# Token loads, product order and half norms of a two-layer diffusion trunk

## The chip, the core and the metric

The kernel runs on one core of one Trainium2 chip. The metric is the device time of one execution in microseconds (us).

## What is computed

One inference step of a diffusion trunk with two layers of width 2048, for 512 latent (sample) and 128 context (prompt) tokens, all in fp32. Each layer normalizes, scales and shifts its input, projects it, runs two mixers with gates, and projects their joined output back into the residual.

```python
def even_mixer(h, w_in, w_out, ...):        # layer 0; layer 1 is odd_mixer, built alike
    qa, ka, va, ga, ub, bb, cb, gb = split_cols(h @ w_in, EVEN_SPLIT)
    q = rms_norm(q_heads(qa, A_KV, A_GROUP), qn)
    ...
    o = banded_attend(apply_rope(q, cos, sin), apply_rope(k, cos, sin), v, ctx[0], ctx[1], sink_g)
    y_a = merge_heads(o) * jax.nn.silu(ga)
    y_b = gated_short_conv(ub, bb, cb, conv_w) * jax.nn.silu(gb)
    return jnp.concatenate([y_a, y_b], axis=-1) @ w_out, new
```

The change touches the projection by `w_out` in both layers, the one by the odd layer's `w_in`, the norm between the layers, and the norm of the queries (`q_heads`).

## The kernel before

All 640 tokens are worked on together. Activations lie transposed, features on the 128 partitions and tokens along the row, so a matrix of 2048 features is 16 tiles of 128x640, and a matmul takes 320 tokens, one of two halves, at a time. Weights stream from memory. [...] A program-wide scheduler takes the written program and orders the instructions of each engine, so that a line's place in the source is not its place in time; buffers come from pools, with a semaphore wait where one is still in use.

`project` does an output projection, and the front of the odd input projection. It starts with three output tiles at once (`run_tiles`), quarter by quarter of the 16 input tiles in the order 0, 2, 1, 3. The four token tiles of a quarter, a unit below, are made by `make_h` just before their use: a tile `yin` of the mixers' output is loaded from memory on SyncE's queue and split into `h`. After that comes one output tile by itself, and the rest goes in pairs (`run_pairs`): two output tiles by two token halves form a 2x2 block product over two halves of the inputs, done with seven products instead of eight from sums of weights and of token tiles. Each product has 24 matmuls. Q1, P6, P7 and P4 add up in one PSUM bank, `pa`; N5 and Q3 share `pb0`; Q2 opens `pb1`. `after` copies what a product leaves for later (L507, L510, L512 for `u2` after P6, L516 for `u3` after P7) and passes finished blocks to `out`. There are 20 pairs: 6 in layer 0's output projection, 8 in the odd layer's front, 6 in layer 1's output projection. Weight sums for them are made on VectorE in place (`sx`, `sf`).

Between the layers, `x1_last` squares the last residual tiles and `norm_half` forms the mean square of one token half with one-column matmuls against `ones`, takes the power on GpSimd, broadcasts it with matmuls against `ident`, and copies it out; only then can the next layer's token tiles of that half be scaled and split (L1318, L1320, L1322).

`q_gen` (it holds L643) norms and rotates the queries while other projections' matmuls run; each `yield` hands the turn to these.

Of the kernel before, what the change touches and what calls it, by code (L numbers as in the profile page):

```python
# [50 lines left out]
def trunk_kernel(ctx: ExitStack, tc: tile.TileContext, I: dict, O: dict):  # L51
# [24 lines left out]
    def close(name):  # L76
        pools.pop(name).__exit__(None, None, None)
# [224 lines left out]
    def drain(queue):  # L302
        while queue:
            advance(queue, 1)
# [139 lines left out]
    def run_pairs(cols, w_ap, mov, room, begin, out, tail):  # L444
# [81 lines left out]
        for i, (p, name) in enumerate(seq):  # L526
# [100 lines left out]
    def q_gen(ap, pp, tag, gain, then=None, wait=True):  # L627
# [11 lines left out]
        V.tensor_add(m, m, sw)  # L639
        yield  # L640
        ss = psT()
# [215 lines left out]

    def y_maker(tags, width, held=()):
        def make(k):
            if k in held:  # L860
                drain(attn)
                t = y[k]
            else:
                t = pools["cur"].tile([P, width], F32, tag=tags[k % len(tags)], name="yin", bufs=4 // len(tags))[:, 0:NT]
                nc.sync.dma_start(t, ydram[k])
            hi, lo = new_h(k)
            split(hi, lo, t)
        return make

# [252 lines left out]

    def late_yin(k):
        t = pools["cur"].tile([P, NT], F32, tag="xr", name="yin", bufs=3)
        nc.sync.dma_start(t, ydram[k])
        split(*new_h(k), t)

    def half_of(k0, i):  # L1130
# [5 lines left out]

    def project(w, cols, n0, maker, job, begin, out, tail, by_half=False):

        go_on = run_tiles([(cols[n], job(n)) for n in range(3)], w, maker, order=(0, 2, 1, 3), by_half=by_half)

# [36 lines left out]

    def project_out(l, maker, finish, last, tail):

# [33 lines left out]

        project(W_OUT[l], [n * P for n in range(KT)], n0, maker, job, begin, out, tail)


    make_y0 = y_maker(("q0h", "q0l", "q1h", "q1l"), NT)

    def mid_tile(n):
        return pools["cur"].tile([P, NT], F32, tag=n, name=n, bufs=1)  # L1220

    def y0_maker(k):
        if k < 4:
            return make_y0(k)
        if k == 8:
            close("even")
            open_pool("mid")
            lay_out("T7 T6 T5 T4 sf xr w8 sx")
            st["acc"], st["sq"] = (mid_tile(n) for n in ("acc", "sq"))
            attn.append(forms())  # L1230
        late_yin(k)

# [11 lines left out]
    def x1_last(t, h):  # L1244
        n, sl = KT - 2 + t, HV[h][1]
        if t != h:
            squares(n, sl)
            return
        nc.gpsimd.dma_start(xdram[n], st["xr", n])
        if h:  # L1250
            g = norm_half(n, h)
            advance([g], 1)
            advance([g], 1)
            drain(prep)
            attn.append(g)
        else:
            prep.append(norm_half(n, h))


    def norm_half(n, h):  # L1260
        sl = HV[h][1]
        A.activation(st["sq"][:, sl], st["xr", n][:, sl], AF.Square)
        yield
        starts = [HALF * h, HALF * h + P, HALF * (h + 1) - P]
# [3 lines left out]
        for i, s in enumerate((st["acc"], st["sq"])):  # L1268
            for b, o in enumerate(starts):
                PE.matmul(tot[:, 4 * i + b:4 * i + b + 1], s[:, o:o + P], ones[:, 0:1], start=True, stop=True)  # L1270
# [26 lines left out]

    project_out(0, y0_maker, x1_done, x1_last, x1_tail)

# [273 lines left out]


    def y1_maker(k):
        if k == 4:
            drain(attn)
            close("odd")
            open_pool("fin")
            lay_out("T7 T6 xr T5 w8 sx sf T4")  # L1580
            attn.append(forms())
        if k % 8 >= 4:
            late_yin(k)
        else:
            t = pools["cur"].tile([P, 768], F32, tag="P", name="yin", bufs=P_BUFS)[:, 0:NT]
            nc.sync.dma_start(t, ydram[k])
            split(*new_h(k), t)

# [12 lines left out]
    def rows_last(t, h):  # L1601

        n = KT - 2 + t
        if not t:
            if h == 0:
                prep.append(rows_later(n))
            return
# [11 lines left out]

    project_out(1, y1_maker, rows_out, rows_last, lambda name: None)  # L1620
    close("fin")
# [48 lines left out]
```

## Time and profile before

| | before |
|---|---|
| median of 3 runs | 2295.69 us (2292.07 to 2299.78) |
| the profiled execution | 2294.4 us |
| its span | 2292.6 us |
| mean granted clock of TensorE | 0.999 |
| TensorE matmuls busy | 2255.9 us (98%) |
| VectorE / ScalarE / GpSimd busy | 1589.8 / 1088.9 / 160.0 us |
| mean traffic | 150 GB/s |

Rows of a timeline read: start in us, length in us, engine, line, operation, what it writes <- what it reads, shapes, and in brackets the idle time of the engine before it with what ended it. A matmul's length is about twice the distance to the next one, since they overlap: distances between starts tell the pace. Rows of the waits read: who waited for whom, us in total, times, longest. Rows of windows give the stretch, its length, busy us and instructions (x) of TensorE's matmuls, its weight loads, VectorE, ScalarE and GpSimd, then the granted clock, the DMA engines' share and GB/s.

### The profile page before, as it was taken

What the parts mean: (1) busy time and instruction counts of PE and PEld (TensorE: products, weight loads), DVE (VectorE), ACT (ScalarE), POOL (GpSimd) and SP (SyncE); (2) the same over time, 40 slices, a digit from 0 to 9 for tenths busy, and PEclk for the clock granted to TensorE, in tenths of its full rate; (3) what the DMA queues carried; (4) which work ended last, traced back from release to release, by engine and by line L of the source; (5) the groups of instructions that cost most, each with busy time, mean ns of one, the idle gap of its engine ahead of it and who ended that gap; (6) DMA issues with size and microseconds to landing.
All of it is one profiled execution on the core that took longest, in us unless ns stands there. A gap on an engine that the chain in (4) does not pass through costs nothing.

```text
span 2292.6 us, 41100 instructions
## 1 busy us (share of the span) xinstructions
PE 2255.9 (98%) x15900; PEld 2178.0 (95%) x15900; DVE 1589.8 (69%) x2831; ACT 1088.9 (47%) x2304; POOL 160.0 (7%) x224
## 2 busy tenths in 40 slices
PE   7999999999999999999999999999999999999999
PEld 5889999999999999999999999999999999999999
DVE  4666968779779776887787665365665655557775
ACT  5325652443522222544464443465565676755443
POOL 1001000000000000000100001011111100000101
PEclk9999999999999999999999999999999999999999
DMA  9985537547367564854553335223223221238642
GB/s 321 294 270 161 158 113 218 152 133 219 116 210 216 177 191 137 277 173 140 164 155 108 116 118 152 79 60 104 79 63 101 71 60 49 76 101 269 184 138 62
DMA packets 380899, 342.89 MB, mean 150 GB/s; under 512 B 16402, under 2 KB 338416, under 8 KB 380192
## 3 DMA queue, kind: packets, MB, share of 16 engines
q1 hardware_dynamic: 366288, 296.00, 43.0%
q0 software_dynamic: 13696, 42.10, 5.4%
q8 instruction: 125, 2.05, 0.4%
q10 hardware_dynamic: 720, 2.16, 0.3%
q14 instruction: 70, 0.57, 0.1%
HBM read 301.27 MB, written 38.93 MB: 148 GB/s over the span
## 4 chain that ended last, share of the span: by engine, by line
PE 85%; DVE 4%; ACT 4%; DMA 3%; issue 3%; POOL 1%; SPq 0%; ACTq 0%; POOLq 0%; DVEq 0%
PE pq L537 7%; PE pq L536 7%; PE pq L535 7%; PE pa L256 6%; PE pa L257 6%; PE pb L256 6%; PE pa L258 6%; PE pb L257 6%; PE pb L258 6%; PE pb L271 2%; PE pb L270 2%; PE pa L270 2%; PE pb L272 2%; PE pa L272 2%; PE pa L271 2%
## 5 line engine op out<-in xcount | busy, mean ns | idle before, releaser
L220 ACT ACTIVATE wh<-raw 128x512 fp32r<-128x512 f32 (+1 forms) x456 | 273.1, 600 | 574.0 <-PE pb L257 406.9
L221 DVE TENSOR_TENSOR wl<-raw,wh 128x512 fp32r<-128x512 f32 (+1 forms) x456 | 295.7, 650 | 212.3 <-ACT wh L220 191.9
L256 PE MATMUL pa<-h,wh 128*128 128x320 f32 x1024 | 325.3, 319 | 4.3 <-ACT h L220 2.0
L257 PE MATMUL pa<-h,wh 128*128 128x320 f32 x1024 | 319.5, 313 | 1.7 <-DVE h L221 0.8
L258 PE MATMUL pa<-h,wl 128*128 128x320 f32 x1024 | 318.2, 311 | 0.9 <-DVE wl L221 0.9
L257 PE MATMUL pb<-h,wh 128*128 128x320 f32 x1024 | 317.1, 310 | 0.0
L258 PE MATMUL pb<-h,wl 128*128 128x320 f32 x1024 | 316.8, 309 | 0.0
L256 PE MATMUL pb<-h,wh 128*128 128x320 f32 x1024 | 316.6, 310 | 0.0
L198 DVE SCALAR_TENSOR_TENSOR acc<-adaw,sT,acc 128x1024 f32<-128x1024 f32 x240 | 299.7, 1276 | 0.0
L256 PEld LDWEIGHTS pa<-h,wh 128*128 128x128 f32 x1024 | 193.1, 189 | 18.3 <-issue 10.0
L257 PEld LDWEIGHTS pa<-h,wh 128*128 128x128 f32 x1024 | 193.3, 189 | 7.6 <-issue 3.3
L535 PE MATMUL pq<-h,wh 128*128 128x320 f32 x640 | 198.7, 311 | 0.4 <-ACT wh L220 0.4
L537 PE MATMUL pq<-h,wl 128*128 128x320 f32 x640 | 198.0, 309 | 0.1
L536 PE MATMUL pq<-h,wh 128*128 128x320 f32 x640 | 197.7, 309 | 0.0
L258 PEld LDWEIGHTS pa<-h,wl 128*128 128x128 f32 x1024 | 193.1, 189 | 3.5 <-issue 2.1
L257 PEld LDWEIGHTS pb<-h,wh 128*128 128x128 f32 x1024 | 192.2, 188 | 1.0 <-issue 0.8
L256 PEld LDWEIGHTS pb<-h,wh 128*128 128x128 f32 x1024 | 192.1, 188 | 0.8 <-issue 0.4
L258 PEld LDWEIGHTS pb<-h,wl 128*128 128x128 f32 x1024 | 192.3, 188 | 0.0
L537 PE MATMUL pq<-T,wl 128*128 128x320 f32 x480 | 147.7, 308 | 0.2 <-DVE wl L221 0.2
L536 PE MATMUL pq<-T,wh 128*128 128x320 f32 x480 | 147.9, 308 | 0.0
L535 PE MATMUL pq<-T,wh 128*128 128x320 f32 x480 | 147.6, 308 | 0.1
L270 PE MATMUL pa<-h,wh 128*128 128x320 f32 x432 | 141.0, 326 | 0.0
(431 smaller groups left out, 5306.0 us busy)
## 6 DMA issues: line engine op xcount, KB each, us to landing
adaw<-in_ada_w SPq DMA_DIRECT2D x128, 512.0 KB, 4.3
raw<-in_ev_w_in SPq DMA_DIRECT2D x176, 256.0 KB, 3.5
raw<-in_od_w_in SPq DMA_DIRECT2D x160, 256.0 KB, 2.9
ada<-in_ada_w SPq DMA_DIRECT2D x32, 1024.0 KB, 7.9
w<-in_od_w_in SPq DMA_DIRECT2D x24, 512.0 KB, 4.0
yd<-y POOLq DMA_DIRECT2D x32, 320.0 KB, 3.2
yin<-yd SPq DMA_DIRECT2D x32, 320.0 KB, 4.5
w<-yd SPq DMA_DIRECT2D x32, 320.0 KB, 4.2
```

Source lines behind the costliest of these rows:

```text
L198: V.scalar_tensor_tensor(out=acc[c], in0=w, scalar=sT[:, kt, c:c + 1], in1=acc[c], op0=ALU.mult, op1=ALU.add)
L220: A.activation(hi, x, AF.Copy)
L221: V.tensor_sub(lo, x, hi)
L256: PE.matmul(ps, wh[:, i, :], hi[:, sl], start=(j == js[0] if alone else (pos == 0 and j == 0)), stop=False)
L257: PE.matmul(ps, wh[:, i, :], lo[:, sl], start=False, stop=False)
L258: last_mm[0] = PE.matmul(ps, wl[:, i, :], hi[:, sl], start=False, stop=(j == js[1] - 1 if alone else (pos == 3 and j == 3)))
L270: PE.matmul(ps, wh[:, j, :], hi[:, sl], start=(qd == 0 and j == 0), stop=False)
L271: PE.matmul(ps, wh[:, j, :], lo[:, sl], start=False, stop=False)
L272: PE.matmul(ps, wl[:, j, :], hi[:, sl], start=False, stop=(qd == 3 and j == 3))
L535: PE.matmul(ps, wh[:, j, :], hi, start=(new and h == 0 and j == 0), stop=False, **kw)
L536: PE.matmul(ps, wh[:, j, :], lo, start=False, stop=False, **kw)
L537: PE.matmul(ps, wl[:, j, :], hi, start=False, stop=(h == 1 and j == 3), **kw)
```

## The change

Four edits, all of order, place and time of issue; no arithmetic is added or taken away.

1. Token loads. `late_yin` and `y_maker` go. A new callback `ahead` of `run_tiles`, called one unit early, loads tiles 8 to 11 into the buffers of attention's probabilities ("P", four of them) and tiles 4 to 6, later 12 to 14, into the three `xr` buffers. It also closes the layer's pool and opens the next before quarter 1; formerly that came with tile 8 in layer 0 and with tile 4 in layer 1. Tiles 7 and 15 are loaded when they are split.
2. Pairs. Q2 moves from fourth to sixth: Q1, N5, P6, P7, Q3, Q2, P4. The next pair's A21 is loaded after P7, A12 and A22 after Q3.
3. Queries. `q_gen` yields once more between the square and the matmuls on it.
4. Norm between the layers. With Q3 earlier, the first half's norm starts a product earlier; the second half's sums are issued behind the latest matmul and its work is spread over more turns. The first residual tiles come back at P7 instead of Q2, except the fourth.

```diff
-        MOV = {"Q1": "B11", "N5": "T1", "P6": "T2", "Q2": "B21", "P7": "T3", "Q3": "B22", "P4": "T4"}
+        MOV = {"Q1": "B11", "N5": "T1", "P6": "T2", "P7": "T3", "Q3": "B22", "Q2": "B21", "P4": "T4"}
...
             elif name == "P7":
+                load(p + 1, "A21")
+            elif name == "Q3":
                 load(p + 1, "A12")
-            elif name == "Q3":
-                load(p + 1, "A21")
                 load(p + 1, "A22")
-            if name in ("Q2", "P7") and p == len(cols) - 1:
+            if name in ("P7", "Q2") and p == len(cols) - 1:
                 tail(name)
...
         V.tensor_add(m, m, sw)
-        yield
+        for _ in range(2):
+            yield
         ss = psT()
...
-    def late_yin(k):
-        t = pools["cur"].tile([P, NT], F32, tag="xr", name="yin", bufs=3)
-        nc.sync.dma_start(t, ydram[k])
-        split(*new_h(k), t)
...
+    def y_ahead(old, new, tags, then=None):
+        def ahead(qd, js):
+            if qd == 2:
+                for k in range(8, 12):
+                    yin_load(k, *P_PLACE)
+                return
+            if qd == 1:
+                drain(attn)
+                close(old)
+                open_pool(new)
+                lay_out(tags)
+                if then:
+                    then()
+                attn.append(forms())
+            for k in range(4 * qd, 4 * qd + 3):
+                yin_load(k, "xr", 3)
+        return ahead
...
     def y0_maker(k):
-        if k < 4:
-            return make_y0(k)
-        if k == 8:
-            close("even")
-            open_pool("mid")
...
-        late_yin(k)
+        yin_split(k, *(("q0h", "q0l", "q1h", "q1l")[k], 1) if k < 4 else ("xr", 3))
...
     def x1_last(t, h):
         n, sl = KT - 2 + t, HV[h][1]
+        if h:
+            nc.gpsimd.dma_start(xdram[n], st["xr", n])
         if t != h:
             squares(n, sl)
-            return
-        nc.gpsimd.dma_start(xdram[n], st["xr", n])
-        if h:
+        elif h:
+            drain(prep)
             g = norm_half(n, h)
-            advance([g], 1)
-            advance([g], 1)
-            drain(prep)
+            next(g)
             attn.append(g)
...
     def norm_half(n, h):
...
-        yield
+        for _ in range(1 + h):
+            yield
...
-            for b, o in enumerate(starts):
-                PE.matmul(tot[:, 4 * i + b:4 * i + b + 1], s[:, o:o + P], ones[:, 0:1], start=True, stop=True)
+            with tc.issue_after(last_mm[0].ins) if h else ExitStack():
+                for b, o in enumerate(starts):
+                    PE.matmul(tot[:, 4 * i + b:4 * i + b + 1], s[:, o:o + P], ones[:, 0:1], start=True, stop=True)
...
     def x1_tail(name):
-        if name == "Q2":
-            for k in range(4):
-                x1_back(k, big("w8", bufs=4))
+        for k in (0, 1, 2) if name == "P7" else (3,):
+            x1_back(k, big("w8", bufs=4))
...
-        if k % 8 >= 4:
-            late_yin(k)
...
+        yin_split(k, *P_PLACE if k < 4 else ("xr", 3))
```

Two places show what the scheduler makes of it. The first is TensorE's order at the end of P6 in the last pair of layer 0. `T_` tiles are sums of token tiles (P6, P7), `h_` tiles are token tiles. Before, Q2 follows, and only its 24 matmuls later P7:

```order
L535 MATMUL pq<-T_11054,wh 128x320
L536 MATMUL pq<-T_11054,wh 128x320
L537 MATMUL pq<-T_11054,wl 128x320
L535 MATMUL pq<-h_10678,wh 128x320 [waits Activation_49]
L536 MATMUL pq<-h_10678,wh 128x320
L537 MATMUL pq<-h_10678,wl 128x320 [waits DVE_49]
L535 MATMUL pq<-h_10683,wh 128x320
```

Now:

```order
L536 MATMUL pq<-T_11078,wh 128x320
L537 MATMUL pq<-T_11078,wl 128x320
L535 MATMUL pq<-h_10670,wh 128x320 [waits Activation_49]
L536 MATMUL pq<-h_10670,wh 128x320
L537 MATMUL pq<-h_10670,wl 128x320 [waits DVE_49]
L535 MATMUL pq<-h_10673,wh 128x320
L536 MATMUL pq<-h_10673,wh 128x320
L537 MATMUL pq<-h_10673,wl 128x320
L535 MATMUL pq<-h_10676,wh 128x320
L535 MATMUL pq<-T_10760,wh 128x320 [waits Activation_49]
L536 MATMUL pq<-T_10760,wh 128x320
```

Seven matmuls of Q3 stand between P6 and P7; the other 17 of Q3 follow P7. The wait for ScalarE ahead of P7 holds the copy of `u2` as well as the weights' split.

The second is TensorE's order at the norm of the second token half, where the next layer has begun (`pa`, `Sp` and `pb` are its first output tiles; `r` is the power's result, broadcast over the partitions). Before:

```order
L258 MATMUL pa<-h_12945,wl 128x320
L1281 MATMUL T<-ident,r_12880 128x128 [waits PE_49,Pool_49]
L1281 MATMUL T<-ident,r_12880 128x128
L1281 MATMUL T<-ident,r_12880 128x64
L257 MATMUL pa<-h_12945,wh 128x320
L258 MATMUL pa<-h_12945,wl 128x320
L257 MATMUL Sp<-h_12933,wh 128x320
L258 MATMUL Sp<-h_12933,wl 128x320
L256 MATMUL Sp<-h_12937,wh 128x320
L257 MATMUL Sp<-h_12937,wh 128x320
L258 MATMUL Sp<-h_12937,wl 128x320
```

Six more rows into `Sp` follow there, then the first into `pb`. Now:

```order
L1281 MATMUL T<-ones,sq 128x1 [waits DVE_49]
L1281 MATMUL T<-ones,sq 128x1 x2
L258 MATMUL pa<-h_12933,wl 128x320
L257 MATMUL Sp<-h_12929,wh 128x320
L258 MATMUL Sp<-h_12929,wl 128x320
L256 MATMUL Sp<-h_12933,wh 128x320
L257 MATMUL Sp<-h_12933,wh 128x320
L258 MATMUL Sp<-h_12933,wl 128x320
L1292 MATMUL T<-ident,r_12951 128x128 [waits Pool_49]
L1292 MATMUL T<-ident,r_12951 128x128
L1292 MATMUL T<-ident,r_12951 128x64
L256 MATMUL pb<-h_12921,wh 128x320 [waits Activation_49]
```

The broadcast of `r` has moved from ahead of thirteen wide matmuls to directly ahead of the first `pb` matmul, and its sums (`ones`) stand six wide matmuls ahead of it. The sums of the first half and their broadcast, which stood in P4 and behind it, now stand in Q2, with P4's 24 matmuls behind them.

More of the change, by code (lines that the diff above doesn't have):

```diff
@@ L856, in save_y, with yin_load, yin_split @@
             nc.gpsimd.dma_start(ydram[k], y[k])
[L858 to L864, printed above, removed]
-                nc.sync.dma_start(t, ydram[k])
-            hi, lo = new_h(k)
-            split(hi, lo, t)
-        return make
+    yin = {}
+    def yin_load(k, tag, bufs, n=NT):
+        yin[k] = pools["cur"].tile([P, n], F32, tag=tag, name="yin", bufs=bufs)[:, 0:NT]
+        nc.sync.dma_start(yin[k], ydram[k])
+    def yin_split(k, *place):
+        if k not in yin:
+            yin_load(k, *place)
+        split(*new_h(k), yin.pop(k))
     xTm = [sp.tile([P, 4 * NT + 1], F32, name=f"xT{g}") for g in range(4)]
@@ L1135, in form_of, with project @@
         return lambda j: (T[j][:, 0, i * HALF:(i + 1) * HALF], T[j][:, 1, i * HALF:(i + 1) * HALF])
-    def project(w, cols, n0, maker, job, begin, out, tail, by_half=False):
-        go_on = run_tiles([(cols[n], job(n)) for n in range(3)], w, maker, order=(0, 2, 1, 3), by_half=by_half)
+    def project(w, cols, n0, maker, job, begin, out, tail, by_half=False, ahead=None):
+        go_on = run_tiles([(cols[n], job(n)) for n in range(3)], w, maker, order=(0, 2, 1, 3), by_half=by_half,
+                          ahead=ahead)
         quarters = [(cols[n], qd) for n in range(3, n0) for qd in range(4)]
@@ L1176, in project, with project_out @@
         drain(prep)
-    def project_out(l, maker, finish, last, tail):
+    def project_out(l, maker, ahead, finish, last, tail):
         n0 = N_SINGLE[l]
@@ L1212, in out, with mid_places @@
             seen.add(n)
-        project(W_OUT[l], [n * P for n in range(KT)], n0, maker, job, begin, out, tail)
-    make_y0 = y_maker(("q0h", "q0l", "q1h", "q1l"), NT)
+        project(W_OUT[l], [n * P for n in range(KT)], n0, maker, job, begin, out, tail,
+                ahead=ahead)
     def mid_tile(n):
         return pools["cur"].tile([P, NT], F32, tag=n, name=n, bufs=1)
-    def y0_maker(k):
-        if k < 4:
-            return make_y0(k)
-        if k == 8:
-            close("even")
-            open_pool("mid")
-            lay_out("T7 T6 T5 T4 sf xr w8 sx")
-            st["acc"], st["sq"] = (mid_tile(n) for n in ("acc", "sq"))
-            attn.append(forms())
-        late_yin(k)
+    def y_ahead(old, new, tags, then=None):
[15 more added lines that the diff above has]
+        return ahead
+    def mid_places():
+        st["acc"], st["sq"] = (mid_tile(n) for n in ("acc", "sq"))
+    P_PLACE = ("P", P_BUFS, 640)
+    y0_ahead = y_ahead("even", "mid", "T7 T6 T5 T4 sf xr w8 sx", mid_places)
+    def y0_maker(k):
+        yin_split(k, *(("q0h", "q0l", "q1h", "q1l")[k], 1) if k < 4 else ("xr", 3))
     def squares(n, sl=slice(0, NT)):
@@ L1572, in trunk_kernel @@
     advance(attn, 1)
+    y1_ahead = y_ahead("odd", "fin", "T7 T6 xr T5 w8 sx sf T4")
     def y1_maker(k):
[L1576 to L1581, printed above, removed]
-        if k % 8 >= 4:
-            late_yin(k)
[L1584 to L1587, printed above, removed]
+        yin_split(k, *P_PLACE if k < 4 else ("xr", 3))
     def rows_out(n):
@@ L1604, in rows_last @@
         if not t:
-            if h == 0:
+            if h:
                 prep.append(rows_later(n))
```

5 lines of the change are left out of this document (2 added, 3 removed).

## Prediction

> **What bounds the kernel now.** I read the engine totals first, then the chain that ended last, then what TensorE (PE) waited for, and only then the timeline at the places that the change touches.
>
> ```profile
> span 2292.6 us, 41100 instructions
> PE 2255.9 (98%) x15900; PEld 2178.0 (95%) x15900; DVE 1589.8 (69%) x2831; ACT 1088.9 (47%) x2304; POOL 160.0 (7%) x224
> PE 85%; DVE 4%; ACT 4%; DMA 3%; issue 3%; POOL 1%; SPq 0%; ACTq 0%; POOLq 0%; DVEq 0%
> PE pa L256 <- ACT h L220: 2.0, 3, 0.8
> PE pa L256 <- DVE gg L1004: 1.6, 1, 1.6
> PE pa L257 <- DVE h L221: 0.8, 3, 0.4
> PE pq L535 <- ACT wh L220: 0.4, 1, 0.4
> ```
>
> PE is busy 98% of the span and carries 85% of the chain. The last four lines are waits of its matmuls (total, times, longest): a token tile's high part (L220) or low part (L221) cost 2.8 us in six waits, and the pairs' products (pq) lost 0.4 us in one. So the change, which leaves the matmuls' number alone, can win only stretches in which PE stands or runs slowly, and can lose by making new ones. The profiled execution took 2294.4 us, 1.8 outside the span; the median of the runs is 2295.7. I count against 2294.4 and put the difference on the median. About 0.3%, 6.9 us, is what a measurement can tell from no change.
>
> **Tokens of layer 0's output projection.** These rows of the PE timeline are the starts around five stalls (start, length, operation, idle time and its releaser).
>
> ```profile
> 926.39 0.31 PE L258 MATMUL pa<-h,wl 128*128 128x320 f32 x1
> 927.14 0.41 PE L256 MATMUL pa<-h,wh 128*128 128x320 f32 x1 [0.44 <-ACT h L220]
> 928.00 0.41 PE L257 MATMUL pa<-h,wh 128*128 128x320 f32 x1 [0.45 <-DVE h L221]
> ...
> 941.28 0.31 PE L258 MATMUL pb<-h,wl 128*128 128x320 f32 x1
> 942.29 0.42 PE L256 MATMUL pa<-h,wh 128*128 128x320 f32 x1 [0.70 <-ACT h L220]
> 942.54 0.31 PE L256 MATMUL pb<-h,wh 128*128 128x320 f32 x1
> 942.69 0.31 PE L258 MATMUL pa<-h,wl 128*128 128x320 f32 x1
> ...
> 952.36 0.31 PE L258 MATMUL pa<-h,wl 128*128 128x320 f32 x1
> 952.90 0.42 PE L257 MATMUL pa<-h,wh 128*128 128x320 f32 x1 [0.22 <-DVE h L221]
> 953.15 0.31 PE L258 MATMUL pa<-h,wl 128*128 128x320 f32 x1
> 954.28 0.42 PE L256 MATMUL pa<-h,wh 128*128 128x320 f32 x1 [0.82 <-ACT h L220]
> 954.53 0.31 PE L257 MATMUL pb<-h,wh 128*128 128x320 f32 x1
> ```
>
> A matmul that waits for nothing starts 0.15 us after the one before it (942.54 to 942.69). Against that the five stalls cost 0.60, 0.71, 0.86, 0.39 and 0.98 us from start to start, 3.54 together, and the matmul behind each comes 0.25 instead of 0.15 later (942.29 to 942.54), some 0.4 more: 3.9. Behind them stand loads:
>
> ```profile
> 941.50 0.74 ACT L220 ACTIVATE h<-yin 128x640 fp32r<-128x640 f32 x1 [2.67 <-DMA yin<-yd]
> 897.41 23.45 SPq L233 DMA_DIRECT2D raw<-in_ev_w_out  x7
> 920.95 1.41 SPq L1127 DMA_DIRECT2D yin<-yd  x3
> ```
>
> ScalarE (ACT) had nothing to do until the token tile had landed, and SyncE's queue (SP) stood 23.45 us at the weights ahead of it, so the first late tiles were asked for at 920.95. In the new order tiles 8 to 11 go to attention's buffers, ahead of those weights; 4 to 6 are asked for at about 921, one unit (the four tiles of one quarter of the rows) before their use at 942, which no landing in these rows overruns. Only tiles 7 and 15 still wait until a buffer is free. I leave one stall of 0.5 us for those and count **-3.4** (ends: -3.9, and -1.9 if both stall like the longest, 0.98). In layer 1 tiles 0 to 3 and 8 to 11 had such places already, and the six waits quoted above leave it about 0.1 us: **-0.1**. The 1.6 us behind gg comes from attention and stays.
>
> **The six products' order.** Formerly Q2's 24 matmuls, in another bank, lay between P6 and P7, which share one. Now P7 must not write before ACT has copied P6's result out (L512), and the new order has only seven matmuls of Q3 between them in 18 of the 20 pairs, five in layer 0's first and two in layer 1's first.
>
> ```profile
> 1012.62 0.31 PE L537 MATMUL pq<-T,wl 128*128 128x320 f32 x1
> 1012.76 0.31 PE L535 MATMUL pq<-h,wh 128*128 128x320 f32 x1
> ...
> 1012.81 0.63 ACT L220 ACTIVATE wh<-sf 128x512 fp32r<-128x512 f32 x1 [1.13 <-PE pq L536]
> 1013.35 0.41 ACT L512 COPY tables<-pq 128x320 f32<-128x320 f32 x1
> ```
>
> P6 ends with the first row, and ACT splits a weight tile before it copies; the copy ends at 1013.76, 1.00 us after the following product's first start. Seven matmuls take 7 x 0.147 = 1.03 us, so the cover is just spent. But P7's weight load waits with it, and behind a wait the next start came 0.10 us late above: I take 0.11 a pair. Five matmuls cover 0.73 and two 0.29, which leaves 0.4 and 0.85. Sum: 18 x 0.11 + 0.4 + 0.85 = **+3.3**. The low end is 0 (the copy goes first, 0.6 us after P6); the high end is one more split of 0.63 ahead of the copy, 12.6 on top. Behind the wait on PE's queue are P7 and everything after, so nothing hides it.
>
> [...]
>
> The loads that change places with it are free as far as these rows tell: A21 and A12 only swap, P7's weights are summed together with P6's, and Q3's in-place sum now has one product between it and P6's splits, where N5's to P6 had none and pq lost 0.4 us in all.
>
> **The norm between the layers.** With Q3 a product earlier, the first token half's norm (mean square by one-column matmuls into T, power on GpSimd (POOL), L1281's broadcast, then ACT copy, VectorE (DVE) scale, ACT split) moves ahead of P4.
>
> ```profile
> 1123.54 0.72 PE L1270 MATMUL T<-ones,acc 128*128 128x1 f32 x6
> 1125.24 0.72 PE L1270 MATMUL T<-ones,sq 128*128 128x1 f32 x6
> 1127.21 0.86 PE L1281 MATMUL T<-ident,r 128*128 128x128 f32 x6
> 1128.96 1.19 PE L1270 MATMUL T<-ones,sq 128*128 128x1 f32 x6 [0.88 <-ACT sq L1262]
> 1130.01 0.88 PE L256 MATMUL pa<-h,wh 128*128 128x320 f32 x2
> 1131.79 0.64 PE L257 MATMUL pa<-h,wh 128*128 128x320 f32 x1 [0.63 <-DVE h L1322]
> 1136.76 0.78 PE L1281 MATMUL T<-ident,r 128*128 128x128 f32 x6
> 1137.34 0.39 PE L257 MATMUL pa<-h,wh 128*128 128x320 f32 x1
> 1139.33 0.52 PE L256 MATMUL pb<-h,wh 128*128 128x320 f32 x2
> ...
> 1130.00:1140.00 10.00, 9.37 (x47) 8.79 (x48) 5.46 (x15) 3.53 (x8) 3.96 (x5) 0.70 1.14 374
> ```
>
> From 1123.54 to 1139.33 are 15.79 us. In them stand 48 wide matmuls (7.05) and six small groups of 0.58 (1136.76 to 1137.34; 3.5), so 5.2 us were lost: about half as idle time, the other half at the lower clock (0.70 in the last row, a stretch of 10 us: 47 matmuls, where 68 fit at 0.147).
>
> Afterwards: the first broadcast needs 1.97 us from its last sum's start (1125.24 to 1127.21), and behind the sum's 0.58 five wide matmuls cover 0.73, so 0.66 is exposed. P4's 24 matmuls (3.5) then cover the way to the first token tiles, which took 2.8 here (1127.21 to 1130.01). The second half's power has six matmuls (0.88) where it needs some 1.4 to 1.5: 0.6. Its way from broadcast to the first pb matmul takes 1.99 us (1137.34 to 1139.33), which thirteen matmuls covered; now pb comes at once: 1.99 exposed. Together 3.25 against 5.2, a gain of 1.95 at full clock. Whether the clock falls again is open. It fell here among stalls of 0.88 and 0.63, and did not behind a longer one alone:
>
> ```profile
> 2070.62 0.31 PE L272 MATMUL pb<-h,wl 128*128 128x320 f32 x1
> 2072.57 0.42 PE L256 MATMUL pa<-h,wh 128*128 128x320 f32 x1 [1.64 <-DVE gg L1004]
> 2072.98 0.31 PE L258 MATMUL pa<-h,wl 128*128 128x320 f32 x1
> ```
>
> The new stalls lie between these cases. I charge a third of the same drop, 0.95: **-1.0**. Ends: -4.7 (the 1.99 and the clock both come out hidden) and +2 (the drop in full, and POOL's token stores of 0.7 each ahead of the second power).
>
> **The query's squares** (matmuls of qsq into T, L643) wait for a split low part, as this row of the waits has it:
>
> ```profile
> PE T L643 <- DVE ptl L221: 1.4, 3, 0.5
> ```
>
> Three waits, 1.4 us, and with the 0.10 us behind each about 1.7. The squares come one step later now, so those that waited have more time; but in the new order the matmuls after attention's transposes are placed differently too, and a wait can form at the work that follows on the squares (root, rotary). I take about a third, **-0.5** (ends: -1.7 with all three gone, and +1, two waits of the longest kind, 0.5, for nothing won).
>
> The sum is -3.4 - 0.1 + 3.3 - 1.0 - 0.5 = -1.7: 2292.7 for the profiled execution, 2294.0 on the median.
>
> **The rivals.** *All of it hides* (chance 0.18): copies go early (0), tokens -3.9, norm -4.7, squares -1.7, layer 1 -0.1: -10.4, 2285.3. For it: a copy that goes ahead of its split ends at 0.6 us, well inside the cover; against it: in the rows the split goes first, and cover and copy are then equal to 0.03 us. *The copy is late* (0.13): in every pair ACT has one more split ahead of L512. P7 then waits 20 x 0.63 = 12.6 longer: 2306.6. The sign turns where the waits at P7 reach 5.0 us (3.3 + 1.7), 0.25 a pair, and they tell from no change at 11.9 (8.6 more), 0.6 a pair. For it: the copy stood behind one split already; against it: a second split needs a weight buffer that only matmuls behind P7 would free. *The clock stays up* (0.16): the norm wins its 1.95: 2293.0. [...] *The change does nothing where it was meant* (0.13): tiles land as late as before, since the early loads push the weights on SP's queue back by as much, so the -3.4 is missing: 2297.4. The order speaks against it: SP stood there 23 us anyway. The forecast itself has 0.40.
>
> **How the numbers follow.** The range runs from 2285, the first rival's value, to 2304, between the forecast and the late copy. Faster than 2288.8 is the first rival with a little of the others, 0.2; slower than 2302.6 the second with its milder forms, 0.14; the rest 0.66.
>
> **What would show it.** Right: no token wait at L256 and L257 between 920 and 960 in the PE timeline; before each P7 a wait for L512's copy of about a tenth of a microsecond, some 20 times; a gap near 2 us between the second broadcast and pb. Wrong: waits of over half a microsecond at P7, a clock below 0.8 in the slice of the norm, or new waits of Q3 for its weights' sum.

## The result, and the profile after

The changed kernel took 2306.09 us (median of 7 runs, 2300.83 to 2308.95); before took 2295.69 beside it. The ratio is 1.0043 [1.0029, 1.0058]: slower by some 10 us, where 2294 and most likely no change were forecast, with a range that ended at 2304. Timed again with a later group it took 2303.57 beside 2296.78, 1.0031 [1.0020, 1.0043]. The profiled execution took 11.7 us longer from first to last instruction.

The page after, its first two lines on TensorE, and from the waits after some rows that are new or larger, at the places that the change touches (L220, on ScalarE, writes the high part of a weight or token tile, L221, on VectorE, its low part; the product of a weight tile and a token tile is three matmuls of these, L256 to L258, L270 to L272 and, in the pairs, L535 to L537):

```profile
span 2304.3 us, 41078 instructions
PE 2257.7 (98%) x15900; PEld 2178.0 (95%) x15900; DVE 1584.8 (69%) x2831; ACT 1087.0 (47%) x2304; POOL 161.9 (7%) x224
PE pq L537 <- DVE wl L221: 4.5, 2, 2.9
PE pq L535 <- ACT wh L220: 2.5, 1, 2.5
PE pa L258 <- DVE wl L221: 2.0, 2, 1.2
PE T L644 <- DVE ptl L221: 2.0, 4, 0.6
PE pb L256 <- ACT h L1330: 1.7, 1, 1.7
PE pa L257 <- DVE h L221: 0.9, 1, 0.9
PE pa L256 <- ACT wh L220: 0.8, 1, 0.8
PE pq L535 <- ACT tables L512: 0.7, 1, 0.7
```

The token waits at L256 have gone, as they were meant to; waits for weights stand in their place. Where the time goes is clearest when the program is cut at fixed matmuls: the first `pa` matmul of the unit in which before's token stalls begin (926.10 there, 312 matmuls ahead of the first product), and the first and last matmul of each group of pairs (a `pq` row each). The lengths in us, worked out from the starts of those rows in each trace:

```
                            up to   to the   6 pairs, norm,  8 pairs  attention,  6 pairs  clock at 0.50
                            926.10  first    odd front's     of the   to layer 1's of       (in 2nd, 3rd,
                                    product  singles         front    first prod. layer 1  6th column)
before                      926.1    50.1     244.6          196.8     714.4      155.6    0, 6.8, 0
changed                     927.0    49.4     248.4          198.4     716.4      159.8    0, 3.4, 0
changed, 2nd profile (e8)   926.1    48.7     245.4          198.5     716.5      160.7    0, 0, 3.4
changed, squares back (e9)  930.1    50.7     245.8          198.5     714.9      161.0    3.4, 0, 3.4
tokens only (e2)            927.4    47.3     243.6          196.8     714.4      156.6    0, 6.8, 0
layer 0's tokens only (e6)  927.6    49.6     242.7          196.8     714.3      155.8    3.4, 3.4, 0
order and norm only (e3)    927.3    50.2     244.7          198.4     714.0      156.6    0, 3.4, 0
order, norm, squares (e1)   927.7    51.4     245.3          198.5     716.3      157.9    0, 3.4, 0
half the sums' loads (e4)   927.4    45.8     243.8          198.4     715.2      158.1    0, 0, 0
sum put behind (e5)         925.7    49.9     244.3          198.5     715.9      158.1    3.4, 3.4, 0
e5, squares back (e11)      929.8    46.9     245.4          198.4     714.5      160.2    0, 3.4, 3.4
layer 1's loads back (e13)  927.1    49.0     248.1          198.5     716.0      157.6    0, 3.4, 0
squares only (e14)          929.5    50.5     243.5          196.8     715.6      156.5    0, 6.8, 0
e11, layer 1's back (e15)   926.8    50.4     243.4          198.5     713.8      157.0    3.4, 0, 0
```

So the second column of before is 976.23 - 926.10. The first column differs by up to 4.4 us, in no order that follows the edits; I make nothing of it. In the others the changed kernel loses 8 to 11 us: nothing to 3 in layer 0 (second and third column together) although its tokens were earlier, 1.6 in the front, 2 around attention, 4 to 5 in layer 1.

The last column is the time in which the granted clock was at 0.50, counted in slices of 1 us. There the starts lie 0.266 us apart instead of 0.147 (eleven rows of the changed kernel, from 1145.02 to 1147.68), so 3.4 us lose 1.5 by the rows. Taken off below are 1.7 for 3.4 us, an estimate from the clock of 0.50 alone and by the rows 0.2 too much; a length with that taken off is called "at full pace". At full pace the changed kernel loses 4.8 and 2.8 us in layer 0 and 4.2 and 3.4 in layer 1, in its two profiles.

Of the changed kernel's stages around layer 0's first pair, this is the windows view (columns as before):

```profile
920.00:930.00 10.00, 10.00 (x70) 10.00 (x69) 3.17 (x5) 3.64 (x6) 0.00 (x0) 1.00 0.81 278
950.00:960.00 10.00, 10.00 (x70) 10.00 (x70) 7.47 (x14) 4.20 (x6) 0.54 (x1) 1.00 1.00 328
960.00:970.00 10.00, 7.16 (x45) 6.37 (x44) 8.49 (x18) 5.69 (x12) 0.71 (x2) 1.00 0.61 202
970.00:980.00 10.00, 8.38 (x57) 8.02 (x56) 9.98 (x19) 3.37 (x6) 0.37 (x1) 1.00 1.00 285
990.00:1000.00 10.00, 7.62 (x52) 7.62 (x53) 7.14 (x12) 2.97 (x6) 0.00 (x0) 1.00 0.35 97
```

From 920 to 960 TensorE has no gap left, with 70 or 71 matmuls in each 10 us. Then come 45 and 57, and 52 from 990. So the time won on the tokens was not lost beside them but behind them, between 960 and 993. The TensorE timeline of the changed kernel shows the stalls (its start at 989.22 is the last one ahead of the longest):

```profile
963.37 0.41 PE L258 MATMUL pa<-h,wl 128*128 128x320 f32 x1 [0.76 <-DVE wl L221]
965.95 0.41 PE L256 MATMUL pa<-h,wh 128*128 128x320 f32 x1 [0.85 <-ACT wh L220]
967.74 0.42 PE L258 MATMUL pa<-h,wl 128*128 128x320 f32 x1 [1.23 <-DVE wl L221]
978.52 0.41 PE L537 MATMUL pq<-h,wl 128*128 128x320 f32 x1 [1.62 <-DVE wl L221]
989.22 0.30 PE L536 MATMUL pq<-h,wh 128*128 128x320 f32 x1
992.38 0.42 PE L537 MATMUL pq<-h,wl 128*128 128x320 f32 x1 [2.86 <-DVE wl L221]
```

VectorE's timeline, and below it SyncE's, shows what the longest waited for:

```profile
990.50 1.23 DVE L480 TENSOR_TENSOR sf<-w,w 128x1024 f32<-128x1024 f32 x1 [1.89 <-DMA w<-in_ev_w_out]
991.64 1.29 DVE L221 TENSOR_TENSOR wl<-sx,wh 128x512 fp32r<-128x512 f32 x2
```

```profile
985.06 0.34 SPq L1116 DMA_DIRECT2D xr<-x0d  x1
985.50 12.75 SPq L451 DMA_DIRECT2D w<-in_ev_w_out  x4
```

Behind the start at 989.22, TensorE stands at the third matmul of Q3 for its low part. That split (991.64) needs nothing that is late; it stands on VectorE's queue behind L480, the sum A11 + A21 of the *next* pair, and that waits for A21, asked for at 985.50 at the earliest.

### The profile page after: what moved, and what is told of

It reads as the page before. It is cut to its first block, busy times and chain, and to the rows that moved or that the text cites. A ratio compares the mean times of both kernels' runs of the same rounds, so it can differ in the third digit from the quotient of the medians.

```text
span 2304.3 us, 41078 instructions
## 1 busy us (share of the span) xinstructions
PE 2257.7 (98%) x15900; PEld 2178.0 (95%) x15900; DVE 1584.8 (69%) x2831; ACT 1087.0 (47%) x2304; POOL 161.9 (7%) x224
## 5 line engine op out<-in xcount | busy, mean ns | idle before, releaser
L220 ACT ACTIVATE wh<-raw 128x512 fp32r<-128x512 f32 (+1 forms) x456 | 273.0, 600 | 541.6 <-PE pb L257 395.5
L221 DVE TENSOR_TENSOR wl<-raw,wh 128x512 fp32r<-128x512 f32 (+1 forms) x456 | 296.1, 651 | 201.6 <-ACT wh L220 181.6
L256 PE MATMUL pa<-h,wh 128*128 128x320 f32 x1024 | 324.0, 317 | 3.8 <-DVE sum L351 1.4
L258 PE MATMUL pa<-h,wl 128*128 128x320 f32 x1024 | 318.0, 311 | 2.1 <-DVE wl L221 2.0
L256 PE MATMUL pb<-h,wh 128*128 128x320 f32 x1024 | 317.2, 310 | 1.7 <-ACT h L1330 1.7
L258 PE MATMUL pb<-h,wl 128*128 128x320 f32 x1024 | 317.3, 310 | 0.0
L256 PEld LDWEIGHTS pa<-h,wh 128*128 128x128 f32 x1024 | 192.2, 188 | 17.4 <-issue 10.2
L537 PE MATMUL pq<-h,wl 128*128 128x320 f32 x640 | 198.2, 310 | 4.5 <-DVE wl L221 4.5
L535 PE MATMUL pq<-h,wh 128*128 128x320 f32 x640 | 198.8, 311 | 2.5 <-ACT wh L220 2.5
L258 PEld LDWEIGHTS pa<-h,wl 128*128 128x128 f32 x1024 | 192.3, 188 | 4.5 <-DVE wl L221 2.9
L256 PEld LDWEIGHTS pb<-h,wh 128*128 128x128 f32 x1024 | 192.4, 188 | 3.1 <-ACT h L1330 1.9
L258 PEld LDWEIGHTS pb<-h,wl 128*128 128x128 f32 x1024 | 192.8, 188 | 0.0
L535 PE MATMUL pq<-T,wh 128*128 128x320 f32 x480 | 149.7, 312 | 0.7 <-ACT tables L512 0.7
L537 PE MATMUL pq<-T,wl 128*128 128x320 f32 x480 | 147.8, 308 | 0.0
L270 PE MATMUL pa<-h,wh 128*128 128x320 f32 x432 | 141.1, 327 | 0.0
```

The costliest lines, as they stand in the source:

```text
L220: A.activation(hi, x, AF.Copy)
L221: V.tensor_sub(lo, x, hi)
L256: PE.matmul(ps, wh[:, i, :], hi[:, sl], start=(j == js[0] if alone else (pos == 0 and j == 0)), stop=False)
L258: last_mm[0] = PE.matmul(ps, wl[:, i, :], hi[:, sl], start=False, stop=(j == js[1] - 1 if alone else (pos == 3 and j == 3)))
L270: PE.matmul(ps, wh[:, j, :], hi[:, sl], start=(qd == 0 and j == 0), stop=False)
L535: PE.matmul(ps, wh[:, j, :], hi, start=(new and h == 0 and j == 0), stop=False, **kw)
```

## The experiments

Two theories first. LOADS: the early tokens make the eight rounds of token sums (`forms`) late, which read 32 tiles again through the same queue. ORDER: the new product order asks for weights too soon. Each run's first number is its median, the second that of before beside it; then comes the ratio of the two kernels' times, mostly with its 95% interval. The ratio is not the quotient of the two medians. Gains and losses below are taken from it where it is named.

**Parts alone.** e1 puts the loads of before back into the changed kernel; e2 has only the new loads; e3 is e1 with the squares of before too (with the order goes an edit of `rows_last`, by which part of layer 1's last rows is handed on at the second token half instead of the first); e4 halves the loads of the token sums:

```diff
             ts = [big("w8", bufs=4)[:, 0:NT] for _ in range(2)]
-            for i in range(2):
-                nc.sync.dma_start(ts[i], ydram[j + 8 * i])
+            t = big("w8", bufs=4)[:, 0:NT]
+            nc.sync.dma_start(t, ydram[j])      # and t is used twice
```

> The changed kernel with the token loads of before (late_yin, y_maker and the pool switch at tile 8); product order, query squares and half norms as changed. Theory LOADS (the tokens' earlier loads delay the eight rounds of token sums behind them, which read 32 tiles again, so that the first pairs' products wait): the stalls of the changed kernel at 962-992 us (8.1 us) and before layer 1's first pair (some 3 us) are gone, the five token stalls (3.5 us) are back; about 2297 us. Theory ORDER (the new product order asks for A21 sooner and puts its sum ahead of Q3's low parts): the waits of L537 for wl, 1.8 and 3.0 us, stay, and with the token stalls back it is about 2309.

Measured: 2302.27 to 2297.25, 1.0015 [1.0005, 1.0025].

> The kernel before with the changed token loads alone; product order, query squares and norms as before. LOADS: the waits at layer 0's fourth tile (962-967, 3.3 us) and at the first pairs stay in some form; against before -3.5 for the tokens, +5 to +8 in layer 0 and +3 in layer 1: 2299 to 2302. ORDER: the tokens' gain shows: about 2292.

Measured: 2296.04 to 2297.25, 0.9990 [0.9980, 1.0000].

> As the first of this group, and the query squares too as before: only product order and half norms changed. Against before: norm -1.6 as the two traces show it, waits at P7 18 x 0.10 + 0.8 + 0.4 = +3.0, so about 2297 by LOADS. The difference to the first run of the group is what the later query squares cost or win; the changed trace has four new waits of 0.6 us at them and lacks three of 0.5 to 0.7, so between 0 and 1 us. ORDER: 2308.

Measured: 2300.07 to 2297.25, 1.0012 [1.0003, 1.0021].

> The changed kernel, whose rounds of token sums (forms) load one tile instead of two and use it twice, in both layers: 16 of 32 loads of 320 KB left out, so the sums are of other data. LOADS: the sums then come early, the waits at 962-992 and at layer 1's first pair are gone while the tokens stay early: 2306 - 8 - 3 = about 2295. ORDER: A21 of the second pair is still asked for at the same place and Q3's low part still stands behind it: at most the 3.3 us at 962-967 go, about 2303.

Measured: 2295.44 to 2297.25, 0.9993 [0.9984, 1.0002].

Neither theory fits. Tokens alone win 2.3 us (ratio 0.9990, with no change at the interval's end), order with norm and squares loses 3.4 (1.0015), and together they lose 7 to 10 (1.0031 and 1.0043): the two parts interfere. The loss of e3, for which LOADS expected none, is 2.8 (1.0012); in its trace the starts at P7 cost 3.9 over the 20 pairs, and the norm wins some 1.1 (below). With lighter token sums (e4) the whole change is no slower than before, which is LOADS' number, and the three waits from 963 to 968 are gone there; but tokens alone, where the sums are as late, came out below before, which it forbade. In e2 the same sum waits for the same weights, on VectorE's timeline, and nobody minds:

```profile
989.83 1.22 DVE L480 TENSOR_TENSOR sf<-w,w 128x1024 f32<-128x1024 f32 x1 [1.46 <-DMA w<-in_ev_w_out]
990.97 0.68 DVE L221 TENSOR_TENSOR wl<-sx,wh 128x512 fp32r<-128x512 f32 x1
991.57 0.48 DVE L1200 TENSOR_TENSOR tables<-pq,tables 128x320 f32<-128x320 f32 x1
```

There Q3's low part is due two products later, since Q2 and P7 come first. Hence theory QUEUE: early tokens make L480 late, and the new order makes what stands behind it urgent.

**The sum put behind (e5), and controls.** e5 adds one constraint to the changed kernel, on each next pair's sum; in layer 0's first pair L480 and Q3's low parts change places:

```diff
-                V.tensor_add(f, a("A11"), a("A21"))
+                with tc.issue_after(q3_v[0].ins) if p else ExitStack():   # q3_v: Q3's last low part
+                    V.tensor_add(f, a("A11"), a("A21"))
```

> The changed kernel with one constraint on VectorE's order: the next pair's sum A11 + A21 (L480) is issued behind Q3's low parts instead of ahead of them; in layer 0's first pair the two change places, elsewhere nothing that waits. Theory QUEUE (early tokens leave A21 of the second pair late, and the new product order makes Q3's low part, queued behind its sum, due two products sooner): the wait of 2.9 us at 992 goes, at most a new one of 1 us at Q2 comes: 2303. Rival (Q3's low part is late because its own weights' sum or split is late): the wait stays, 2306.

Measured: 2300.00 to 2296.78, 1.0016 [1.0007, 1.0025], with the changed kernel at 2303.57 in the same group. Its trace has no wait between 985 and 992; the low parts come at their time and the sum after them:

```profile
986.54 0.69 DVE L223 TENSOR_TENSOR wl<-sx,wh 128x512 fp32r<-128x512 f32 x1 [0.18 <-ACT wh L222]
987.58 0.69 DVE L223 TENSOR_TENSOR wl<-sx,wh 128x512 fp32r<-128x512 f32 x1 [0.35 <-ACT wh L222]
988.19 1.22 DVE L483 TENSOR_TENSOR sf<-w,w 128x1024 f32<-128x1024 f32 x1
```

(L483 and L223 in this kernel are L480 and L221 of the changed one.) So the wait of 2.4 to 2.9 us is shown to be that place in the queue. At full pace, layer 0's second and third column together are 291.3 in before, 287.5 with the tokens alone (e2) and 293.2 with the order and the norm alone (e3). If these added, the changed kernel would be at 289.4; it is at 296.1 and 294.1, and e5 at 290.8. So in layer 0 the parts interfere by 5 to 7 us, and the sum's place is 3 to 5 of them. A little of the gain lies in layer 1: 158.1 here, and 158.5 at full pace in e11, which has the same constraint, for 159.8 and 159.0.

The other half of QUEUE, that the early tokens make L480 late, explains only part. Counted from the first product, L480 begins at 12.1 us in e3, which has the new order and the old loads, and at 14.2 and 12.3 in the changed kernel's two profiles. What differs is what VectorE has ahead of it. In e3:

```profile
988.96 0.68 DVE L221 TENSOR_TENSOR wl<-sx,wh 128x512 fp32r<-128x512 f32 x1
989.56 1.22 DVE L480 TENSOR_TENSOR sf<-w,w 128x1024 f32<-128x1024 f32 x1
```

One of Q3's two low parts stands ahead of the sum there (in e1 as well), and TensorE does not wait at Q3; in the changed kernel both stand behind it. The scheduler, given other loads, ordered VectorE otherwise. Why it did was not followed.

> The kernel before with the changed token loads in layer 0 alone. The tokens-only run showed in layer 0 a gain of 3.9 us less waits of 2.7, and in layer 1 0.6 more waits at tokens and 1.1 more before the first pair, 1.1 less at attention's end. If those of layer 1 come from its loads, this is at or a little under the tokens-only run: about 2295 beside a before of 2297. If layer 0 alone makes no gain: 2297.

Measured: 2294.94 to 2296.78, 0.9991 [0.9983, 1.0000]. Together with e2 (0.9990), from which it cannot be told apart, this is the best version found, and its gain is barely clear of none. In its profile waits that cost 2.1 us at 964 to 967 have eaten much of the tokens' gain.

> Control: the kernel before with the rounds of token sums loading one tile instead of two (16 of 32 loads left out, sums of other data). Theory: before does not wait for these sums, since its late tokens give them time, so at most the token stalls (3.5) shrink with the emptier DMA: 2294 to 2297 beside 2297. If lighter loads help any version alike, it is 11 us faster, as the changed kernel was: 2286.

Measured: 2292.41 to 2296.78, 0.9981 [0.9972, 0.9990]. Lighter sums are worth 4.4 us to before, and 8 to 11 to the changed kernel: about half of what e4 won belongs to the change.

> The changed kernel again, for a second profile and a time beside the others of this group: 2306. The waits at L256 to L258 between 962 and 968 (3.3 us in the first profile, 1.0 in the tokens-only run, whose order is the same there) follow landing times, so between 1 and 3.5; the wait of some 3 us at 992 stays within 1 us.

Measured: 2303.57 to 2296.78, 1.0031. Its waits:

```profile
PE pq L535 <- ACT wh L220: 4.1, 2, 2.3
PE pq L537 <- DVE wl L221: 2.6, 2, 2.4
PE pa L258 <- DVE wl L221: 0.7, 1, 0.7
```

At the fourth tile 0.7 us are left of 2.8, and the first product waits in its place (1.7 of the 4.1); the wait at Q3 is there again (2.4). So the first kind moves from run to run, as landing times would make it, which is not shown; the second stays.

**Further undoing.** e9 has the squares of before, e11 that and e5's constraint; e10 is e6 with the residual tiles loaded on GpSimd's queue; e12 is e11 with the same.

```diff
-        nc.sync.dma_start(st["xr", n], ...)
+        nc.gpsimd.dma_start(st["xr", n], ...)
```

> The changed kernel with the query squares as before (one yield). The first group put the later squares at +2.2 us (2302.3 against 2300.1) and the traces at four new waits of 0.6 against three of 0.5 to 0.7. If that is real: 2 us under the changed kernel's 2303.6 to 2306.1, about 2302.5. If it is only scatter: the same, 2304.5.

Measured: 2306.73 to 2296.54, 1.0042 [1.0029, 1.0056]: no gain. The attention column fell to 714.9, but the first column grew to 930.1, which was not followed.

> The kernel with layer 0's token loads alone changed (2294.9 beside a before of 2296.8), and the residual tiles xr loaded on GpSimd's queue instead of SyncE's, where they stood blocked for a buffer ahead of the token sums' tiles and of weights (SP idle 958.06 to 963.20 ahead of an xr load). Theory QUEUE: the waits left at 964-978 (2.4 us) shrink to under 1: 2293. Rival LANDING (the transfers themselves are slow while the DMA engines are full): they stay, 2295.

Measured: 2299.60 to 2296.54, 1.0016 [1.0007, 1.0025]: worse than e6 by 4.7, against both. The waits at the fourth tile did go, but in its profile layer 1's first products waited 3.3 us for weights, and the clock stood at 0.50 for 10.2 us around attention and in layer 1's pairs, where it did not in e6's; why was not followed.

> The changed kernel with the next pair's sum behind Q3's low parts (which gave 2300.0 beside a before of 2296.8) and the query squares as before: if both effects add, 2298; then what is left against before is the waits at P7 (some 2) and at the first pairs (some 3), less the norm's 1.6 and part of the tokens' 3.5.

Measured: 2301.40 to 2296.54, 1.0022 [1.0012, 1.0032]: the effects do not add; it is no faster than e5 (1.0016).

> As the run before it in this group, with the residual tiles on GpSimd's queue: by QUEUE the waits at the fourth tile and before the first pairs shrink, 2295 to 2296, below before; by LANDING 2298.

Measured: 2305.07 to 2296.54, 1.0042 [1.0028, 1.0056]. The residual loads are no mend. Its profile, too, has the clock at 0.50 for 3.4 us around attention and for 3.4 in layer 1's pairs.

**Layer 1 and the squares.**

> The changed kernel with layer 1's token loads as before; all else changed. From layer 1's first product to its last row the changed traces take 159.8 and 160.7 us, before 155.6, order alone 156.6, tokens alone 156.6. If the early tokens and the new order together make layer 1's token sums late (interaction, as in layer 0): about 157, the whole about 2301. If the order alone does it there: 159.5 or more, 2304.

Measured: 2301.94 to 2297.32, 1.0019 [1.0009, 1.0029]; layer 1's pairs took 157.6. At full pace they took 156.6 with the order alone (157.9 with the squares too, e1), 156.6 with the loads alone, and 159.8, 159.0 and 159.3 with both (two profiles and e9). Over before's 155.6 that is 2.0 to 3.3 for the two apart and 3.4 to 4.2 together: in layer 1 they mostly add, and interfere by 2 us at most. In the changed kernel the second product there, N5, stood for its weights:

```profile
2143.38 0.39 PE L564 MATMUL T<-ident,xr 128*128 128x128 f32 x2
2146.31 0.42 PE L535 MATMUL pq<-h,wh 128*128 128x320 f32 x1 [2.54 <-ACT wh L220]
```

Ahead of it, on VectorE and, in the second fence, on ScalarE:

```profile
2142.85 1.16 DVE L221 TENSOR_TENSOR T<-sx,T 128x960 fp32r<-128x960 f32 x1
2144.91 1.29 DVE L475 TENSOR_TENSOR sx<-w,raw 128x512 f32<-128x512 f32 x2
```

```profile
2145.63 0.63 ACT L220 ACTIVATE wh<-sx 128x512 fp32r<-128x512 f32 x1 [2.19 <-DVE sx L475]
```

N5's weight sum (L475, VectorE) comes behind the last of the eight token sums (2142.85), and that one came late. In before that sum's split on ScalarE began 1.3 us ahead of layer 1's first product, here 1.9 behind it. N5's wait was 0.2 us in e3, 1.1 in e13, 1.5 in e2, and 2.5 and 2.3 in the changed kernel's two profiles: the early loads alone make about half of it.

> The kernel before with the later query squares alone. In the traces the stretch from the odd front's last product to layer 1's first product takes 715.2 to 716.5 us in the six versions with them and 714.0 to 714.9 in the six without. If the edit does that by itself: the stretch 716, and 2 us over before, about 2298.5; if it only goes with the new order: 714.4 and no difference.

Measured: 2298.11 to 2297.32, 1.0002 [0.9992, 1.0012]; the attention column 715.6. The four new waits, of 0.43 to 0.56 us, at the squares are in its trace, so the edit makes them by itself, worth 1.2 us in the trace and too little for the times to tell.

> The changed kernel with the next pair's sum behind Q3's low parts, layer 1's token loads as before and the query squares as before: new order, norm and layer 0's early tokens remain. If the parts add up: 2301.4 (the run with the first and the third) less some 3 in layer 1, about 2298.5; left over before are the waits at P7 (20 x 0.2 = 4) and at the first pairs, less the norm's and part of the tokens' gain. If layer 1 does not depend on its loads: 2301.

Measured: 2297.11 to 2297.32, 0.9999 [0.9990, 1.0008]. This is within 1.4 us of the sum, so the sum's place and layer 1's loads account for most of the loss; that the squares' part adds is not shown, since taking it back won nothing in e9 and e11. With all three mended, the new order, its norm and layer 0's early tokens are together worth nothing measurable.

## Why the prediction was wrong

The step that failed is that the sum takes each term by itself, and gives what lies between them no term at all: the loads and sums that change places "are free as far as these rows tell". Apart, the loads came out at -2.3 (forecast -3.5) and the order with norm and squares at +3.4 (forecast +1.8); together they cost 7 to 10. So 6 to 9 us come from the two meeting, most of them in layer 0. The terms one by one:

**Tokens, -3.4.** The stalls went, as reckoned: counted from one matmul of the even layer, the changed kernel was 4.4 us ahead of before at 72 matmuls ahead of the first product. But a stall's end was taken for a gain without asking what is late next. It was the token sums. VectorE stood for their loads, with the fourth tile's low parts behind it in its queue:

```profile
960.96 0.49 DVE L1085 TENSOR_TENSOR sf<-w 128x320 f32<-128x320 f32 x1 [2.23 <-DMA w<-yd]
```

Both profiles of the changed kernel, e2, e5, e6, e13 and e15, all with layer 0's early loads, have such a wait, of 1.3 to 2.7 us, between 957 and 961. Before, e1 and e3, with the old loads, have none there, and e4, with half of the sums' loads, has none. Of the eight sums the last one's split on ScalarE began in before and in the changed kernel at:

```profile
970.63 1.01 ACT L220 ACTIVATE T<-sx 128x960 fp32r<-128x960 f32 x1 [0.41 <-DVE sx L1085]
```

```profile
973.96 1.01 ACT L220 ACTIVATE T<-sx 128x960 fp32r<-128x960 f32 x1 [3.34 <-DVE sx L1084]
```

That is 5.6 us ahead of before's first product (976.23) and 2.4 ahead of the changed one's (976.35). The sums' loads came later: SyncE's queue asked for the last of them at 959.55 and 960.56 in before and at 963.62 in the changed kernel, where it had stood still from 958.06 to 963.20 ahead of a residual tile. That they set the pace up to the first product is what e4 says: its second column is 45.8 us, 312 matmuls at 0.147, so nothing is lost there. The tokens' own gain was as reckoned: 3.8 at full pace in e2's second and third column.

**Layer 1, -0.1.** Layer 1's pairs took 3.4 to 4.2 us more at full pace. About 1.9 of these are the waits at P7 there, which the order's term counts; of the rest N5's wait is the greater part. It is the same step: only the token waits were weighed, and the sums behind the moved loads were not.

**Order, +3.3.** The wait at P7 was foreseen and is there in the TensorE timeline, in layer 0's second pair and in layer 1's first:

```profile
1017.70 0.30 PE L535 MATMUL pq<-h,wh 128*128 128x320 f32 x1
1017.94 0.42 PE L535 MATMUL pq<-T,wh 128*128 128x320 f32 x1
1018.19 0.31 PE L536 MATMUL pq<-T,wh 128*128 128x320 f32 x1
...
2155.04 0.42 PE L535 MATMUL pq<-T,wh 128*128 128x320 f32 x1 [0.65 <-ACT tables L512]
```

P7's start is 0.24 after its forerunner and the next 0.25 after it, against 0.147: 0.2 us a pair, not 0.11. The front's eight pairs took 196.8 in every version with the old order and 198.4 or 198.5 in every one with the new, 1.6 for 8. Layer 1's first pair, with two matmuls ahead of P7, lost 0.9 (0.85 reckoned); layer 0's first, with five, lost nothing (0.4 reckoned). So the term is 18 x 0.2 + 0.9 = 4.5, mechanism right, size low by a quarter. What failed beside it is "the loads that change places with it are free": that argument looked at Q3's own sum and not at the next pair's sum ahead of Q3's low part, which cost 2.4 to 2.9 us. Among the signs of being wrong "new waits of Q3 for its weights' sum" were named; it was another sum in front of it.

**Norm, -1.0.** Held as far as the table can tell: e3's third column equals before's (244.7 to 244.6) with six waits at P7 in it, 1.2 us, so the norm won about 1.1. The waits were foreseen one by one (0.66, 0.6 and 1.99), and 0.5, 0.4 and 2.0 came; the last two, in the timeline and the window of the changed kernel:

```profile
1139.94 0.31 PE L258 MATMUL Sp<-h,wl 128*128 128x320 f32 x1
1140.46 0.88 PE L1292 MATMUL T<-ident,r 128*128 128x128 f32 x6 [0.21 <-POOL r L1286]
1143.09 0.56 PE L256 MATMUL pb<-h,wh 128*128 128x320 f32 x2 [1.75 <-ACT h L1330]
```

```profile
1140.00:1150.00 10.00, 8.04 (x44) 7.65 (x43) 7.14 (x21) 6.94 (x17) 0.41 (x1) 0.83 1.02 312
```

From broadcast to pb 2.63 us pass, of which 2.0 are lost; and the clock fell again in this profile, to 0.83 in that slice (0.70 before). The second profile of the same kernel (e8) has the same gap and no fall, with a clock of 1.00 from 1136 to 1146:

```profile
1139.64 0.57 PE L256 MATMUL pb<-h,wh 128*128 128x320 f32 x2 [1.75 <-ACT h L1330]
```

All eleven traces with the new norm have the same gaps here (0.37 or 0.38, 0.2 and 1.75). In six of them the clock fell to 0.50 for 3.4 us (this one, e1, e3, e5, e11, e12), in five it did not fall (e4, e8, e9, e13, e15). With the old norm it fell in all six, for 6.8 us in five and 3.4 in e6. So the risk, charged at 0.95, came as 1.5 (by the rows) to 1.7 (by the clock) in about half the traces, and these gaps alone do not decide which. Of the 1.1 that the norm won in e3, the shorter fall is 1.5 to 1.7: its waits cost some 0.4 to 0.6 more than before's. (Before's 5.2 lost were then 3.0 to 3.4 of clock and 1.8 to 2.2 of idle time, not half and half.) One bound of the working does not follow from its rows: with the 1.99 and the clock both hidden, 5.2 - 0.66 - 0.6 = 3.9 is won and not 4.7, and the first rival would be at 2286.1.

**Squares, -0.5.** Wrong in sign in the trace: 1.2 us more in e14's, too little for its times to show. Waits of 0.4 to 0.5 went at three queries and waits of 0.43 to 0.59 came at four others, which the end "+1" had allowed for.

**The rivals.** None was this one. *All of it hides* would have needed P7 free of waits, which cost 4.5. *The copy is late* named nearly the time that was measured (2306.6), by chance: P7 stayed at 0.2 a pair, and the loss lies elsewhere. *The clock stays up* held in five traces of eleven, and is worth 1.5 to 1.7 us. *The change does nothing where it was meant* had the early loads push other loads back, but expected the tokens themselves to be late; they were not, and what was late were the sums behind them.

## What to carry to other kernels

Where the token stalls went (3.9 us), TensorE ran up to the next supply that was hidden behind them (it stood 2.8 us at layer 0's fourth tile): when a stall goes, follow the loads and sums that share its queue and DMA, and compare their times with when they will now be due. When work is moved earlier, look at what stands *ahead* of it on every queue, the next round's work included (here L480 ahead of L221), since a scheduler may have put that there while there was room. Two edits that cost little alone can meet at one place (here -2.3 and +3.4 became 7 to 10), and a scheduler that sees the whole program may order other engines anew for either, so each part's trial has to be read beside the whole.

## What was not expected of the hardware

The changed kernel waited 2.8 and 0.7 us at layer 0's fourth tile in two profiles of the same program: a single trace did not give that wait's size. A wait at P7 of less than a tenth (0.24 between starts, at 1017.94, instead of 0.147) costs twice that, 0.2, since the next start comes 0.10 late as well (0.25, at 1018.19).

Where the clock fell, it fell to 0.50 for 3.4 us or twice that, and the 10 us windows show only the mean (0.83 for 3.4 us, from 1140). The gap before it does not tell whether it falls: after the 1.75 us at the norm it fell in six traces of eleven, with the same rows around it; after Q3's gap of 2.9 us it fell in e13 (at 992), and after 2.86 us it stayed at 1.00 in the changed kernel's first profile (at 992 too). A fall of 3.4 us costs 1.5 to 1.7 us, as much as many a term of the sum, so stage lengths of two traces should be compared only after looking at the clock in slices of 1 us.
